# One tile of a depthwise convolution: from GpSimd to the tensor engine, by way of four shifted copies in DRAM

## The chip, the core and the metric

The kernel runs on one core of a Trainium2 chip. Its time is the device time of one execution in microseconds (us); less is better. A core has a tensor engine (PE), a vector engine (DVE), a scalar engine (ACT), GpSimd (POOL), and a queue (SP) that only starts DMA transfers; ACT and POOL start a few as well. Each engine works through its own list of instructions in the order in which the program puts them, and waits on semaphores for the others.

## The reference

One layer of a streaming encoder, for 512 tokens of width 1024, all in float32. A convolution module and an attention module run on one projected input, share one output projection, and a mixture of 32 experts follows. The part that changes is the depthwise convolution over time, 31 taps for each of 512 channels, causal:

```
CONV_CH = 512; CONV_K = 31; SEQ = 512
proj = h @ w_in
conv_val, conv_gate, c_q, c_kv, k_rope = jnp.split(proj, [o1, o2, o3, o4], axis=-1)
...
u  = val * jax.nn.sigmoid(gate)
dw = lax.conv_general_dilated(u, kern, window_strides=(1,), padding=[(CONV_K - 1, 0)],
        dimension_numbers=("NWC", "WIO", "NWC"), feature_group_count=CONV_CH) + conv_b
y_conv = jax.nn.silu(layer_norm(dw, ln_g, ln_b))
...
mixed = jnp.concatenate([y_conv, y_attn], axis=-1) @ w_out
x = x + g_a[:, None] * mixed
return x + g_f[:, None] * hier_moe(rms_norm(x) modulated ...)     # 32 experts, top 2 of one group
```

## The kernel before

The 512 channels are four tiles of 128 channels on the partitions, with time (512) along the row. `conv_in(t, pv, pg)` forms `u` of tile t from two PSUM banks (value and gate): ACT takes a tanh (L312), DVE forms (tanh + 1) * value (L318, or L315 for the tensor engine's tile). The taps of the four tiles are shared out:

- Tiles 0 and 2 are DVE's: `conv_taps` is 31 instructions a tile (L343, L345), each a multiply-add over 128x512. They are put between other DVE work a few at a time by calls of `tap(n)`.
- Tile 1 is GpSimd's: in `conv_taps_pool` ACT multiplies a shifted slice by its tap (L355), GpSimd adds the product to `dw` (L357); 30 adds and 31 ACT instructions, put in by `tap(n, ptaps)`: 3 after each of the four steps of `conv_pair(2)`, 2 after each step of `conv_pair(3)`, and 1 with each of the first attention scores.
- Tile 3 is the tensor engine's: `conv_in` stores `u` to a DRAM buffer `ud` (L316, a DMA on ACT's queue), `load_rep` loads four copies of it, each shifted by one more step, onto the four quarters of the partitions (L325, four DMAs on SP's queue), and `conv_mm` runs 8 steps of four matmuls of 128x32 by 512 (L333), each step covering four taps. The bank is evicted by ACT (L336). The tap weights for it are spread over 32x32 blocks once, by GpSimd (`cwb`, L304).

The order of the program around this: a sweep over the input projection fills tiles 0's banks and the latent columns; then `conv_pair(1)`, `conv_pair(2)`, `conv_pair(3)` compute the value and gate banks of tiles 1 to 3 (16 steps of three matmuls each, L117 to L119). Between their steps stand single steps of `ada_rest` (matmuls L585, whose 1 MB weight pieces SP loads one after another into a ring of four buffers, L511), `c_chunk(0)` to `c_chunk(2)`, and the DVE taps. A `c_chunk` is four PE transposes into a bank of the two-bank pool `tr` (L643), an ACT eviction (L646), an ACT cast (L647) and a DVE subtraction (L648). `pair_split(3)`, two ACT casts (L378) and two DVE subtractions (L379), stands before `conv_pair(2)` in the program and makes the weights that `conv_pair(3)` uses. After `conv_pair(3)` come four rounds of `qkv_mm`/`qkv_tr` (keys, queries and values of 128 tokens: DVE L762 to L785 with taps between them, GpSimd's rotary products L550 to L553 and a root L194), then 32 steps of attention: `scores` (PE L877, DVE L878 and L879, ACT L881), `p_tr` (PE L891), and after every eighth step `attn_out` (PE L901, L909). From the eighth step on the output weights are split (DVE L839, GpSimd L841). Then the output projection, the routing and the experts, whose weights stream in over SP's queue as buffers come free.

PE, DVE, ACT, SP and (up to the end of attention) POOL run in the order of the program. A DMA that an engine's queue starts stands in that engine's order too: the queue goes on only when the DMA's semaphores are there.

Of the kernel before, what the change touches and what calls it, by code (L numbers as in the profile page):

```python
# [37 lines left out]
CONV_POOL, CONV_PE = (1,), 3  # L38
# [3 lines left out]
def hybrid_block(ctx: ExitStack, tc: tile.TileContext, A, out, dbg=None, stop=None):  # L42
# [31 lines left out]
    PP2, PP3, PPQ, PPA = 3, 2, 0, 1  # L74
# [214 lines left out]
    u = S([128, 3, 542])  # L289

    ud = dram.tile([129, 544], F32, tag="ud", name="ud")
    cwb = S([128, 32, 32])
    rep = []

    def conv_setup():
        zz = rp[:, 512:608]
        pool.memset(zz, 0.0)
        pool.dma_start(ud[:, :32].rearrange("(p a) b -> p a b", a=3), zz[:43].rearrange("p (a b) -> p a b", a=3))
# [5 lines left out]
        pool.tensor_tensor(cwb, m32[:, None, :].to_broadcast([128, 32, 32]),  # L304
                           col("cwp")[:, :, None].to_broadcast([128, 32, 32]), op=OP.mult)
# [15 lines left out]
    def load_rep():  # L321
        rep.append(C([128, 4, 540], name="u", uname="rep"))
        flat = ud.rearrange("a b -> (a b)")
        for i in range(4):
            sp.dma_start(rep[0][32 * i:32 * i + 32],  # L325
                         flat[2 + i:2 + i + 128 * 544].rearrange("(g c s) -> c g s", c=32, s=544)[:, :, :540])

    def conv_mm():

        p = fb()  # L330
        for k in range(8):
            for g in range(4):
                pe.matmul(p[32 * g:32 * g + 32, :], cwb[:, 8 * g + k, :], rep[0][:, g, 4 * k:4 * k + 512],  # L333
                          start=(k == 0), stop=(k == 7), tile_position=(0, 32 * g), skip_group_check=True)
            if k == 7:
                act.activation(dw[:, CONV_PE, :], p, AF.Identity, bias=col("cb", CONV_PE, CONV_PE + 1))  # L336
            yield

    def conv_taps(t):
        for k in range(31):  # L340
            w = cwh[:, 31 * t + k:31 * t + k + 1]
            if k == 0:
                dve.tensor_scalar(dw[:, t, :], u[:, t, 0:512], w, col("cb", t, t + 1), op0=OP.mult, op1=OP.add)  # L343
            else:
                dve.scalar_tensor_tensor(dw[:, t, :], u[:, t, k:k + 512], w, dw[:, t, :], op0=OP.mult, op1=OP.add)  # L345
            yield

    def conv_taps_pool(t):

        z = [rp[:, 0:512], rp[:, 896:1408]]  # L350
        for k in range(32):
            if k == 0:
                act.activation(dw[:, t, :], u[:, t, 0:512], AF.Identity, scale=cwh[:, 31 * t:31 * t + 1], bias=col("cb", t, t + 1))
            elif k < 31:
                act.activation(z[k % 2], u[:, t, k:k + 512], AF.Copy, scale=cwh[:, 31 * t + k:31 * t + k + 1])  # L355
            if k > 1:
                pool.tensor_tensor(dw[:, t, :], dw[:, t, :], z[(k - 1) % 2], op=OP.add)  # L357
            yield

    taps, ptaps = [], []  # L360

    def tap(n, q=None):
        q = taps if q is None else q
# [293 lines left out]
    for k in range(4):  # L657
        run(g, 4)
        fill(F2[k])
        if k < 3:  # L660
            c_chunk(k)
        tap(P2)
        tap(PP2, ptaps)
    run(g)
    g = conv_pair(3)
    for k in range(4):
# [3 lines left out]
        tap(PP3, ptaps)  # L670
    run(g)

# [136 lines left out]
    conv_steps, CM = conv_mm(), (0, 1, 1, 0)  # L809
# [5 lines left out]
    for tt in range(4):  # L815
        nxt_ = qkv_mm(tt + 1, g) if tt < 3 else None
        if tt == REP_AT:
            load_rep()
# [3 lines left out]
        tap(PPQ, ptaps)  # L822
# [831 lines left out]
def pack(inputs):  # L1654
# [73 lines left out]
```

## Time and profile before

| | before |
|---|---|
| median of three runs (lowest, highest) | 550.88 us (549.04, 552.13) |
| the profiled execution, its span | 550.6 us, 549.0 us |
| PE busy | 486.6 us, 89% |
| DVE busy | 298.5 us, 54% |
| ACT busy | 197.3 us, 36% |
| POOL busy | 169.2 us, 31% |
| HBM read | 149.84 MB |

The span runs from the first to the last instruction; 1.6 us of the time lie outside it. Busy shares are means over stages with different limits, and PE's busy time is modelled, so a busy PE is not PE at its peak. All times in rows below are from the start of the span.

### The profile page before, as it was taken

The page shows a single profiled execution, that of the slowest core. Times are in us where ns is not written, and L with a number is a line of the kernel's source. Part 1 is how long each engine was busy: PE and PEld are TensorE (multiplying, and loading weights), DVE is VectorE, ACT ScalarE, POOL GpSimd, SP SyncE. Part 2 cuts the span into 40 slices and gives each one's busy share as a digit, 9 for nine tenths or more (in the row PEclk, how much of TensorE's full clock was granted, in tenths as well). Part 3 has the DMA queues.
Part 4 walks back from the last instruction along what each step waited for, and adds up shares of the span by engine and source line. Part 5 has one row for each costly group of instructions (what it writes and reads, how often), then busy time and mean ns, then how long its engine had stood idle before and what let it go on. Part 6 is the DMA issues. An engine that isn't in the chain of part 4 may idle for free.

```text
span 549.0 us, 8137 instructions
## 1 busy us (share of the span) xinstructions
PE 486.6 (89%) x2827; PEld 277.8 (51%) x2827; DVE 298.5 (54%) x631; ACT 197.3 (36%) x419; POOL 169.2 (31%) x147
## 2 busy tenths in 40 slices
PE   4999999948988979999998999999999789989962
PEld 3778865534643446688884443443434332424321
DVE  2447699998998676662456333436433231415532
ACT  4233754534578556752443513112221020211000
POOL 3110674975889563110000213112221120101100
PEclk9999999968999889999999989999999989999988
DMA  8999536935971234266959889999999999999972
GB/s 249 299 347 304 182 131 257 381 113 179 231 217 67 78 93 149 78 236 213 367 180 382 291 346 335 347 409 413 373 414 408 410 411 415 408 410 303 327 296 96
DMA packets 60946, 153.00 MB, mean 279 GB/s; under 512 B 7485, under 2 KB 27085, under 8 KB 55264
## 3 DMA queue, kind: packets, MB, share of 16 engines
q1 hardware_dynamic: 57712, 145.91, 74.7%
q0 software_dynamic: 1792, 3.97, 2.1%
q10 hardware_dynamic: 1392, 2.51, 1.3%
q8 instruction: 24, 0.39, 0.3%
q14 instruction: 26, 0.21, 0.1%
HBM read 149.84 MB, written 4.49 MB: 281 GB/s over the span
## 4 chain that ended last, share of the span: by engine, by line
PE 46%; DVE 23%; DMA 20%; ACT 3%; SPq 3%; issue 2%; POOL 1%; ACTq 0%; DVEq 0%; POOLq 0%
DVE dw L345 10%; PE acc L1480 10%; DMA s<-in_w_up_e_dram 9%; PE acc L1506 6%; PE f L1523 5%; DMA w<-in_w_up_e_dram 4%; PE acc L117 4%; PE acc L119 3%; PE acc L118 3%; DMA w<-in_w_down_e_dram 3%; DMA s<-in_w_down_e_dram 2%; DMA s<-in_w_ada_dram 2%; PE acc L909 2%; DVE sm L879 2%; PE acc L877 1%
## 5 line engine op out<-in xcount | busy, mean ns | idle before, releaser
L1480 PE MATMUL acc<-s,gw 128*32 128x512 f32 (+1 forms) x392 | 93.3, 604 | 1.5 <-DMA s<-in_w_up_e_dram 1.5
L117 PE MATMUL acc<-s,s 128*128 128x512 f32 (+3 forms) x160 | 64.8, 405 | 10.7 <-DVE s L318 8.2
L345 DVE SCALAR_TENSOR_TENSOR dw<-s,cwh,dw 128x512 f32<-128x512 f32 x60 | 63.6, 1061 | 1.5
L119 PE MATMUL acc<-s,s 128*128 128x512 f32 (+3 forms) x160 | 60.1, 376 | 1.4 <-DVE s L379 1.4
L118 PE MATMUL acc<-s,s 128*128 128x512 f32 (+3 forms) x160 | 60.1, 376 | 0.0
L1523 PE MATMUL f<-s,t 128*128 128x512 f32 x184 | 48.7, 412 | 10.8 <-DVE t L1462 8.1
L1480 PE MATMUL acc<-w,gw 128*32 128x512 f32 (+1 forms) x136 | 53.5, 619 | 4.1 <-DMA w<-in_w_up_e_dram 4.0
L1485 DVE TENSOR_TENSOR t<-t,acc 128x256 f32<-128x256 f32 x12 | 5.1, 421 | 91.0 <-ACT t L1483 91.0
L1511 POOL TENSOR_TENSOR s<-t,s 128x512 fp32r<-128x512 f32 x22 | 28.5, 1295 | 75.9 <-ACT s L1510 75.9
L1483 ACT ACTIVATE t<-acc 128x256 f32<-128x256 f32 x12 | 4.6, 384 | 127.8 <-PE acc L1480 127.8
L1480 PEld LDWEIGHTS acc<-s,gw 128*32 128x32 f32 (+1 forms) x392 | 25.8, 123 | 47.9 <-issue 46.4
L357 POOL TENSOR_TENSOR dw<-dw,s 128x512 f32<-128x512 f32 x30 | 45.6, 1518 | 13.1 <-ACT s L355 11.4
L1526 DVE TENSOR_TENSOR s<-s,f 128x512 f32<-128x512 f32 x52 | 35.2, 687 | 20.0 <-PE f L1523 20.0
L1506 PE MATMUL acc<-s,t 128*32 128x512 f32 (+1 forms) x200 | 45.3, 609 | 0.5 <-ACT t L1494 0.5
L1523 PEld LDWEIGHTS f<-s,t 128*128 128x128 f32 x184 | 31.1, 188 | 26.9 <-DVE s L1526 7.3
L1438 POOL DMA_INDIRECT s<-xg,sidx x11 | 11.2, 1020 | 106.9 <-PE tr L1454 65.5
L117 PEld LDWEIGHTS acc<-s,s 128*128 128x128 f32 x160 | 31.1, 194 | 25.2 <-DVE s L318 8.6
L1510 ACT CAST s<-t 128x512 fp32r<-128x512 f32 x24 | 14.8, 618 | 54.8 <-DVE t L1509 54.8
L119 PEld LDWEIGHTS acc<-s,s 128*128 128x128 f32 x160 | 31.1, 194 | 5.9 <-DVE s L379 1.8
L118 PEld LDWEIGHTS acc<-s,s 128*128 128x128 f32 x160 | 31.2, 195 | 3.4 <-issue 0.2
L1509 DVE SCALAR_TENSOR_TENSOR t<-acc,rt,gw 128x512 f32<-128x512 f32 x24 | 18.0, 751 | 27.0 <-PE acc L1506 27.0
L881 ACT ACTIVATE t<-acc,sm,qs 128x128 f32<-128x128 f32 (+3 forms) x32 | 19.7, 616 | 19.9 <-DVE sm L879 16.6
(313 smaller groups left out, 856.1 us busy)
## 6 DMA issues: line engine op xcount, KB each, us to landing
s<-in_w_down_e_dram SPq DMA_DIRECT2D x21, 1024.0 KB
s<-in_w_gate_e_dram SPq DMA_DIRECT2D x41, 512.0 KB
s<-in_w_up_e_dram SPq DMA_DIRECT2D x41, 512.0 KB
w<-in_w_ada_dram SPq DMA_DIRECT2D x16, 1024.0 KB
w<-in_w_gate_e_dram SPq DMA_DIRECT2D x15, 512.0 KB
w<-in_w_up_e_dram SPq DMA_DIRECT2D x15, 512.0 KB
w<-in_w_down_e_dram SPq DMA_DIRECT2D x7, 1024.0 KB
s<-in_w_ada_dram SPq DMA_DIRECT2D x6, 1024.0 KB
```

The costliest lines, as they stand in the source:

```text
L117: pe.matmul(o, lh, rh, start=start, stop=False)
L118: pe.matmul(o, lh, rl, start=False, stop=False)
L119: pe.matmul(o, ll, rh, start=False, stop=stop)
L345: dve.scalar_tensor_tensor(dw[:, t, :], u[:, t, k:k + 512], w, dw[:, t, :], op0=OP.mult, op1=OP.add)
L357: pool.tensor_tensor(dw[:, t, :], dw[:, t, :], z[(k - 1) % 2], op=OP.add)
L881: act.activation(e[:, :n], p[:, :n], AF.Exp, scale=qs[:, qt, h:h + 1], bias=H["nb"][:, qt:qt + 1], accum_out=H["rs"][:, qt:qt + 1])
L1480: pe.matmul(gu[sl, :], self.hg[:, j, sl], w.t[:, :, j % 4, :], start=(j == 0), stop=(j == 7), tile_position=(0, o_), skip_group_check=True)
L1506: pe.matmul(o[o_:o_ + w_, :], self.aT[:, n * c + o_:n * c + o_ + w_], w.t[:, c, hs], start=(c == 0), stop=(c == 1), tile_position=(0, o_), ...
L1509: dve.scalar_tensor_tensor(yf[:n], o[:n], self.gate, gf[:n, hs], op0=OP.mult, op1=OP.mult)
L1511: eng.tensor_tensor(self.yhl[:n, 1, hs], yf[:n], self.yhl[:n, 0, hs].bitcast(F32), op=OP.subtract)
L1523: pe.matmul(o, u_.ot[:u_.n, tt * 128:(tt + 1) * 128], u_.yhl[:u_.n, k, 512 * hf:512 * hf + 512], start=(m == 0 and k == 0), stop=(m == len ...
L1526: dve.tensor_tensor(xr, xr, o, op=OP.add)
```

## The change

Tile 1 is treated as tile 3 was. `conv_taps_pool` and its queue go, with all 30 adds of GpSimd and 31 instructions of ACT. `conv_in(1)` now forms `u` in a temporary and stores it to a second DRAM buffer, `ud1`; four loads on SP fill `rep1`; `conv_mm(1)` runs right after `conv_pair(3)`, all 8 steps in one piece. The block weights `cwb` double, from 128x1024 to 128x2048. `rep1` and `rep3` share one buffer in SBUF. DVE's two tiles stay.

```diff
-CONV_POOL, CONV_PE = (1,), 3
+CONV_PE = 1, 3
...
     def conv_in(t, pv, pg):
...
-        if t == CONV_PE:
+        if t in CONV_PE:
             ut = T()
             dve.scalar_tensor_tensor(ut, th, 1.0, pv, op0=OP.add, op1=OP.mult)
-            act.dma_start(ud[:128, 32:], ut)
+            act.dma_start(ud[t][:128, 32:], ut)
             return
-        dve.scalar_tensor_tensor(u[:, t, 30:], th, 1.0, pv, op0=OP.add, op1=OP.mult)
-        (ptaps.append(conv_taps_pool(t)) if t in CONV_POOL else taps.append(conv_taps(t)))
+        dve.scalar_tensor_tensor(u[:, t // 2, 30:], th, 1.0, pv, op0=OP.add, op1=OP.mult)
+        taps.append(conv_taps(t))
...
-    def conv_taps_pool(t):
-        z = [rp[:, 0:512], rp[:, 896:1408]]
-        for k in range(32):
-            if k == 0:
-                act.activation(dw[:, t, :], u[:, t, 0:512], AF.Identity, scale=cwh[:, 31 * t:31 * t + 1], bias=col("cb", t, t + 1))
-            elif k < 31:
-                act.activation(z[k % 2], u[:, t, k:k + 512], AF.Copy, scale=cwh[:, 31 * t + k:31 * t + k + 1])
-            if k > 1:
-                pool.tensor_tensor(dw[:, t, :], dw[:, t, :], z[(k - 1) % 2], op=OP.add)
-            yield
...
     g = conv_pair(2)
     for k in range(4):
         run(g, 4)
         fill(F2[k])
         if k < 3:
             c_chunk(k)
+        if k == 2:
+            load_rep(1)
         tap(P2)
-        tap(PP2, ptaps)
     run(g)
     g = conv_pair(3)
+    conv_steps = conv_mm(1)
     for k in range(4):
         run(g, 4)
         fill(F3[k])
         tap(P3)
-        tap(PP3, ptaps)
     run(g)
+    run(conv_steps)
...
             scores(i // 4, i % 4)
             tap(PT)
-            tap(PPA, ptaps)
```

On ACT, behind the tanh of tile 1 (t_766 before, t_768 now), stood the casts of `pair_split(3)` (s_773) and the eviction and cast of `c_chunk(0)` (tr_797), then the first products of GpSimd's tile. Before:

```order
L312 ACTIVATE t_766<-f_701 128x512
L378 CAST s_773<-w_574 128x1024 x2
L646 ACTIVATE t_802<-tr_797,smalls 128x512
L647 CAST s_634<-t_802 128x512
L353 ACTIVATE dw<-s_147,smalls,cwh 128x512
L355 ACTIVATE s_146<-s_147,cwh 128x512 x2
L646 ACTIVATE t_836<-tr_831,smalls 128x512
```

And of the change, the same place:

```order
L312 ACTIVATE t_768<-f_703 128x512
L316 DMA ud_148<-t_770 128x512
L367 CAST s_777<-w_576 128x1024 x2
L635 ACTIVATE t_806<-tr_801,smalls 128x512
L636 CAST s_636<-t_806 128x512
L635 ACTIVATE t_836<-tr_831,smalls 128x512
```

The store of `u` of tile 1 (t_770, which DVE writes) now stands ahead of the casts and of the first `c_chunk`'s eviction, and the products of GpSimd's tile are gone.

On PE, at the end of `conv_pair(3)` (acc_905), the matmuls of `conv_mm(1)` come ahead of the first key matmuls of `qkv_mm` (acc_1048). Of the change:

```order
L574 MATMUL f_988<-w_959,cs 32x512 x4
L116 MATMUL acc_905<-s_140,s_777 128x512
L117 MATMUL acc_905<-s_142,s_777 128x512
L118 MATMUL acc_905<-s_140,s_778 128x512
L334 MATMUL f_1006<-rep_870,s_150 32x512 x32
L116 MATMUL acc_1048<-s_692,s_636 128x512
```

In the kernel before the last three matmuls of `conv_pair(3)` and the key matmuls follow each other directly; the 32 in one row are new.

On SP, the loads of `rep1` (rep_870) stand among the 1 MB pieces of `ada_rest`. Of the change:

```order
L500 DMA w_859<-in_w_ada_dram 128x2048
L325 DMA rep_870<-ud_148 32x4x540 x4
L500 DMA w_894<-in_w_ada_dram 128x2048
L500 DMA w_919<-in_w_ada_dram 128x2048
L500 DMA w_939<-in_w_ada_dram 128x2048
```

Before, the pieces followed each other with nothing between; the loads of `rep3` stay where those of `rep` were.

## Rows read from the trace of the kernel before

**Rows 1.** The page's fourth part: shares of the chain that ended last

```profile
DVE dw L345 10%; PE acc L1480 10%; DMA s<-in_w_up_e_dram 9%; PE acc L1506 6%; PE f L1523 5%; DMA w<-in_w_up_e_dram 4%; PE acc L117 4%; PE acc L119 3%; PE acc L118 3%; DMA w<-in_w_down_e_dram 3%; DMA s<-in_w_down_e_dram 2%; DMA s<-in_w_ada_dram 2%; PE acc L909 2%; DVE sm L879 2%; PE acc L877 1%
```

**Rows 2.** DVE and POOL in the timeline: start, length, line, operation, [idle before]

```profile
69.77 17.07 DVE L345 SCALAR_TENSOR_TENSOR dw<-s,cwh,dw 128x512 f32<-128x512 f32 x15
86.76 0.68 DVE L318 SCALAR_TENSOR_TENSOR s<-t,f 128x512 f32<-128x512 f32 x1
...
91.30 4.53 DVE L379 TENSOR_TENSOR s<-w,s 128x1024 fp32r<-128x1024 f32 x2
...
97.45 5.17 DVE L345 SCALAR_TENSOR_TENSOR dw<-s,cwh,dw 128x512 f32<-128x512 f32 x3
...
120.93 5.47 DVE L345 SCALAR_TENSOR_TENSOR dw<-s,cwh,dw 128x512 f32<-128x512 f32 x7
...
88.98 31.62 POOL L357 TENSOR_TENSOR dw<-dw,s 128x512 f32<-128x512 f32 x18 [9.78 <-ACT s L355]
```

**Rows 3.** PE in the timeline, 76 to 125 us

```profile
86.54 0.65 PE L643 MATMUL tr<-ident,t 128*128 128x128 f32 x4
...
93.66 0.50 PE L119 MATMUL acc<-s,s 128*128 128x512 f32 x1 [1.36 <-DVE s L379]
...
109.28 1.06 PE L585 MATMUL f<-w,cs 128*32 128x512 f32 x8
110.27 0.50 PE L117 MATMUL acc<-s,s 128*128 128x512 f32 x1
...
120.14 0.69 PE L117 MATMUL acc<-s,s 128*128 128x384 f32 x1 [8.20 <-DVE s L318]
...
124.27 1.48 PE L585 MATMUL f<-w,cs 128*32 128x512 f32 x8
```

**Rows 4.** ACT in the timeline (ACTq: a DMA that its queue starts)

```profile
75.10 1.98 ACT L378 CAST s<-w 128x1024 fp32r<-128x1024 f32 x2
78.22 0.69 ACT L646 ACTIVATE t<-tr,smalls 128x512 f32<-128x512 f32 x1 [1.14 <-PE tr L643]
...
127.03 0.37 ACTq L316 DMA_DIRECT2D ud<-t  x1
127.45 0.60 ACT L759 ACTIVATE t<-acc 128x512 f32<-128x512 f32 x1 [7.28 <-DVE t L315]
```

**Rows 5.** Windows: length, busy us of PE, PEld, DVE, ACT, POOL, granted clock, DMA

```profile
114.00:116.00 2.00, 0.00 (x0) 0.00 (x0) 1.96 (x2) 1.05 (x2) 1.92 (x2) 0.73 0.00 0
...
124.00:126.00 2.00, 1.75 (x10) 0.20 (x8) 1.89 (x4) 0.00 (x0) 0.00 (x0) 0.71 0.51 213
```

**Rows 6.** SP's queue in the timeline, the four loads of `rep`

```profile
137.60 4.62 SPq L325 DMA_DIRECT2D rep<-ud  x4
```

**Rows 7.** POOL and DVE in the timeline, the first `qkv_mm`

```profile
129.26 1.22 POOL L550 TENSOR_TENSOR t<-s,s 128x256 f32<-128x256 f32 x1 [8.65 <-DVE sm L190]
...
135.00 0.69 DVE L783 TENSOR_TENSOR s<-acc,ks 128x512 f32<-128x512 f32 x1 [1.08 <-POOL ks L194]
```

**Rows 8.** POOL in the timeline, its first work behind the block weights

```profile
56.94 6.17 POOL L379 TENSOR_TENSOR s<-w,s 128x1024 fp32r<-128x1024 f32 x2 [17.66 <-ACT s L378]
```

**Rows 9.** PE in the timeline, attention: scores of steps 4, 12, 20, 28, and one `attn_out`

```profile
165.62 0.49 PE L877 MATMUL acc<-s,s 100*128 100x128 f32 x2
...
181.36 0.80 PE L877 MATMUL acc<-s,s 100*128 100x128 f32 x2
...
199.02 0.41 PE L877 MATMUL acc<-s,s 100*128 100x128 f32 x2
...
200.44 1.98 PE L901 MATMUL tr<-ident,rec 128*64 128x128 f32 x16 [0.68 <-DVE s L892]
...
205.18 0.70 PE L877 MATMUL acc<-s,s 100*128 100x256 f32 x2
...
215.19 0.39 PE L877 MATMUL acc<-s,s 100*128 100x128 f32 x2
```

**Rows 10.** Waits of SP's queue, longest first: us in total, times, longest

```profile
SPq L1008 <- POOL s L841: 40.2, 3, 22.5
```

More of the change, by code (lines that the diff above doesn't have):

```diff
@@ L73, in hybrid_block @@
     P2, P3, PQ = 3, 2, 2
-    PP2, PP3, PPQ, PPA = 3, 2, 0, 1
     REP_AT = 1
@@ L288, in hybrid_block @@
     rp = S([128, 2048])
[L289 to L293, printed above, removed]
+    u = S([128, 2, 542])
+    ud = {t: dram.tile([129, 544], F32, tag=f"ud{t}", name=f"ud{t}") for t in CONV_PE}
+    cwb = S([128, 64, 32])
+    rep = {}
     def conv_setup():
@@ L297, in conv_setup @@
         pool.memset(zz, 0.0)
-        pool.dma_start(ud[:, :32].rearrange("(p a) b -> p a b", a=3), zz[:43].rearrange("p (a b) -> p a b", a=3))
+        for t in CONV_PE:
+            pool.dma_start(ud[t][:, :32].rearrange("(p a) b -> p a b", a=3), zz[:43].rearrange("p (a b) -> p a b", a=3))
         m32 = rp[:, 608:640]
@@ L303, in conv_setup @@
         dve.tensor_scalar(m32, m32, 0.5, None, op0=OP.mult)
-        pool.tensor_tensor(cwb, m32[:, None, :].to_broadcast([128, 32, 32]),
-                           col("cwp")[:, :, None].to_broadcast([128, 32, 32]), op=OP.mult)
+        pool.tensor_tensor(cwb, m32[:, None, :].to_broadcast([128, 64, 32]),
+                           col("cwp")[:, :, None].to_broadcast([128, 64, 32]), op=OP.mult)
     def conv_in(t, pv, pg):
@@ L312, in conv_in, with load_rep, conv_mm @@
         act.activation(th, pg, AF.Tanh, scale=0.5)
-        if t == CONV_PE:
+        if t in CONV_PE:
             ut = T()
             dve.scalar_tensor_tensor(ut, th, 1.0, pv, op0=OP.add, op1=OP.mult)
-            act.dma_start(ud[:128, 32:], ut)
+            act.dma_start(ud[t][:128, 32:], ut)
             return
-        dve.scalar_tensor_tensor(u[:, t, 30:], th, 1.0, pv, op0=OP.add, op1=OP.mult)
-        (ptaps.append(conv_taps_pool(t)) if t in CONV_POOL else taps.append(conv_taps(t)))
-    def load_rep():
-        rep.append(C([128, 4, 540], name="u", uname="rep"))
-        flat = ud.rearrange("a b -> (a b)")
+        dve.scalar_tensor_tensor(u[:, t // 2, 30:], th, 1.0, pv, op0=OP.add, op1=OP.mult)
+        taps.append(conv_taps(t))
+    def load_rep(t):
+        rep[t] = C([128, 4, 540], name="u", uname=f"rep{t}")
+        flat = ud[t].rearrange("a b -> (a b)")
         for i in range(4):
-            sp.dma_start(rep[0][32 * i:32 * i + 32],
+            sp.dma_start(rep[t][32 * i:32 * i + 32],
                          flat[2 + i:2 + i + 128 * 544].rearrange("(g c s) -> c g s", c=32, s=544)[:, :, :540])
-    def conv_mm():
+    def conv_mm(t):
+        w0 = 32 * CONV_PE.index(t)
         p = fb()
@@ L332, in conv_mm @@
             for g in range(4):
-                pe.matmul(p[32 * g:32 * g + 32, :], cwb[:, 8 * g + k, :], rep[0][:, g, 4 * k:4 * k + 512],
+                pe.matmul(p[32 * g:32 * g + 32, :], cwb[:, w0 + 8 * g + k, :], rep[t][:, g, 4 * k:4 * k + 512],
                           start=(k == 0), stop=(k == 7), tile_position=(0, 32 * g), skip_group_check=True)
             if k == 7:
-                act.activation(dw[:, CONV_PE, :], p, AF.Identity, bias=col("cb", CONV_PE, CONV_PE + 1))
+                act.activation(dw[:, t, :], p, AF.Identity, bias=col("cb", t, t + 1))
             yield
@@ L342, in conv_taps, with tap @@
             if k == 0:
[L343 removed]
+                dve.tensor_scalar(dw[:, t, :], u[:, t // 2, 0:512], w, col("cb", t, t + 1), op0=OP.mult, op1=OP.add)
             else:
[L345 removed]
+                dve.scalar_tensor_tensor(dw[:, t, :], u[:, t // 2, k:k + 512], w, dw[:, t, :], op0=OP.mult, op1=OP.add)
             yield
[L348 to L363 removed]
+    taps = []
+    def tap(n):
+        q = taps
         while n and q:
@@ L807, in qkv_tr @@
                 yield i
-    conv_steps, CM = conv_mm(), (0, 1, 1, 0)
+    conv_steps, CM = conv_mm(3), (0, 1, 1, 0)
     QS = 3
@@ L817, in hybrid_block @@
         if tt == REP_AT:
-            load_rep()
+            load_rep(3)
         tap(PQ if tt < 3 else T3[2])
@@ L821, in hybrid_block @@
             run(conv_steps, CM[0])
-        tap(PPQ, ptaps)
         for i, _ in enumerate(qkv_tr(tt, tok)):
@@ L1677, in pack @@
     put("cw", cw.transpose(2, 1, 0).reshape(128, 124))
-    cp = np.zeros((32, 4, 32), np.float32)
-    cp[:31] = cw[:, CONV_PE].reshape(31, 4, 32)
-    put("cwp", cp.reshape(8, 4, 4, 32).transpose(1, 3, 2, 0).reshape(128, 32))
+    cps = []
+    for t in CONV_PE:
+        cp = np.zeros((32, 4, 32), np.float32)
+        cp[:31] = cw[:, t].reshape(31, 4, 32)
+        cps.append(cp.reshape(8, 4, 4, 32).transpose(1, 3, 2, 0).reshape(128, 32))
+    put("cwp", np.concatenate(cps, 1))
     put("qa", nat(g["q_a_norm"][0]))
```

2 lines of the change are left out of this document (1 added, 1 removed).

## The prediction

> **What bounds the kernel now.** I read the page's chain first, then the timelines of DVE, POOL, PE and ACT over one stretch, 60 to 230 us, because outside it the change touches only some preparation before 40 us. In the chain the reader should see that DVE's taps and the expert matmuls lead with a tenth of the span each, and that the expert weights (the DMA entries) come next [rows 1]: there is no one bound, each stage has its own. GpSimd's adds do not appear in the chain at all. What the change can save must therefore come through something that they hold up.
>
> They hold up DVE. While GpSimd adds, from 88.98 for 31.62 us, three of DVE's taps take 5.17 us, 1.72 each; when GpSimd rests, seven take 5.47 us, 0.78 each [rows 2]. Because DVE is late, PE stands for 8.20 us in front of 120.14, waiting for DVE's L318, and then works at half clock [rows 3]: the granted clock was already falling in 114 to 116, with PE idle, and only in 124 to 126 it was on its way back [rows 5].
>
> **The change, step by step.** I follow the in-order lists through this stretch, on the profiled execution (550.6 us; the median of the runs, 550.88, is 0.3 above it, which I neglect).
>
> *DVE.* Between 95.8 and 119.4 stand 14 instructions of 128x512 (11 taps, 3 subtractions of `c_chunk`) at about 1.7, which come to about 0.78: 14 x 0.92 = 12.9 us, and the two L379 take 4.53 now [rows 2] and some 2.5 without company (an estimate: two of twice a tap's length less a fixed part). DVE gets some 15 us of room. But what stands behind its taps waits for PE, so this room is worth only what PE's order lets through.
>
> *The store moved ahead on ACT.* ACT's queue now holds at the store of `ud1` until DVE has written tile 1, and that is L318 at 86.76, behind 15 taps [rows 2]. Nothing of GpSimd's tile slows these 15 taps, so they stay where they are. Queued behind the store are the two casts of `pair_split(3)` and the eviction of `c_chunk(0)`, which ran at 75.10 and 78.22 [rows 4]. Now: 86.76 + 0.68 = 87.44, store 0.37, casts 1.98, eviction 0.69 [rows 2, 4], so `c_chunk(0)` leaves its bank at 90.5. The transposes of `c_chunk(2)` need that bank, since the pool has two, and PE reached them at 86.54 [rows 3]. PE is in order, so it stands there for 4.0 us. That the queue really holds is in the trace: behind the store of tile 3, ACT stood for 7.28 us on DVE's L315 [rows 4].
>
> *The clock.* A pause of 4 us may let the clock fall. Before, PE stood for 8.20 us, and with the clock at half until about 125 it worked some 5 us at 1.2 GHz after 120.14, worth 2.5 us [rows 3, 5]. The new pause is half as long and the work behind it denser: bounds 0 (no fall) and 2.5, and I take 1.7, nearer to the row of a pause that did cost. The Trainium skill, in "TensorE: Matmul & The Clock Gate", Part 1, says that the throttled state is the default and that sustained activity alone releases it, which speaks against a change that puts a new hole into a stretch where PE had none; by it the term would be the full 2.5 and the sum 0.8 us worse. The trace agrees in kind (0.73 in 114 to 116) [rows 5].
>
> *What falls away on PE.* `conv_pair(3)` stood 1.36 us for L379 [rows 3]. PE now comes there some 5.7 us later and DVE is done by 93, so the wait goes. `conv_pair(3)` therefore ends at about 111.1 + 4.0 + 1.7 - 1.4 = 115.4 (its last three matmuls start at 110.27 [rows 3] and take 0.8).
>
> *The 32 matmuls.* One step of four has the shape of an L585 step, which takes 0.99 us from start to start (109.28 to 110.27 [rows 3]): 8 x 0.99 = 7.9 us, to 123.3. They fill the 8.20 us in which PE stood for DVE. Without that cover they would cost the full 7.9. Their input: `rep1` can start when the store has landed, which no row times; from below nothing, from above the four loads of `rep`, issued over 4.62 us from 137.60 [rows 6] and used without a wait at 156.5, so at most 19 us. Issued at about 91, `rep1` is there by 110 at the worst, ahead of 115.4. The 1 MB pieces behind it on SP are needed from about 104 on; the same bound lets one of them be late by 2 us at most, and I take 0.
>
> *The first `qkv_mm`.* Keys 0.8, then twelve query matmuls, which took 120.14 to 124.27 at half clock [rows 3] and take about 2.1 at full: PE has them at 126.2. ACT copies them in about 0.6, and GpSimd's rotary products, at 129.26 before, start at 126.8: 2.5 us earlier. They release L783 on DVE, at 135.00 before [rows 7]. From there up to attention DVE is the bound in both kernels, with the same work, so the lead is kept: **front part 2.5 us, bounds 0.5 and 4.3** (clock term and 1 us either way in the pause).
>
> *Attention.* Steps 4 to 12 took 15.7 us with GpSimd's adds and ACT's products among them (165.62 to 181.36); steps 20 to 28, with neither, and almost without splitting of output weights, 16.2 less one `attn_out` of 4.7 (200.44 to 205.18), so 11.4 [rows 9]. The gain is between 0 and 4.3. The four casts and subtractions of the output weights in it stay, and so do the matmuls of tile 3, so I take half, 2.0, and 0.6 for steps 0 to 4: **2.6 us, bounds 0 and 5**.
>
> *Costed at nothing:* the doubled `cwb` on GpSimd, since GpSimd stands 17.66 us before its next work at 56.94 [rows 8]; the second clearing store beside it; 16 KB more of small inputs. If that cover were gone, the price would be about one GpSimd instruction of 128x1024, 3.1 us [rows 8].
>
> *Behind attention* everything is released by work that moves along: the first expert loads wait 40.2 us in three waits for GpSimd's L841 [rows 10]. So the lead arrives whole at the end. Sum: 550.6 - 2.5 - 2.6 = **545.5 us**.
>
> **The rivals.** *All of DVE's room counts.* If PE did not bind from 86 to 123, 15 us of front and 2.6 of attention would come through: 533. For it speaks that DVE's taps lead the chain [rows 1]; against it, that PE stands only 1.36 and 8.20 us in the whole stretch [rows 3], and 4.0 plus 7.9 are put in. The Trainium skill, in "SBUF — State Buffer", Who interferes with whom, has the shared read port held for a whole instruction by a DVE operation with two SBUF inputs or by GpSimd, the loser blocked; by that the 15 us are truly freed on DVE. The trace agrees (1.72 against 0.78). A part of this, down to 541, is possible if the pause is shorter. Chance 0.10.
>
> *The lead is lost on the way:* the clock stays down longer than 2.5 us are worth, attention keeps its pace because PE's own work sets it (0 from rows 9's lower bound), or the weight stream of the last 300 us does not move. Front 0.5, attention 0: 550.1. Chance 0.20.
>
> *Slower: the taps do not quicken.* If DVE's 1.72 has another cause than GpSimd, DVE still reaches L318 of tile 2 at about 119.5, then eight more taps at 1.7, and L315 at 133. The second store on ACT holds the queue until then, with the eviction of `conv_mm(1)` and the key squares behind it: 133.7 instead of 127.45, 6.2 us later, less 2.6 in attention: 554.2. It decides once L315 comes after 124. Against it speak the seven taps at 0.78 with DMA running beside them [rows 2, 5]. Chance 0.07; for causes that I do not see, above 553, another 0.06.
>
> **How the numbers follow.** The forecast, 541.5 to 548.1, has 0.57. I count 0.5% (2.75 us), about what a measurement of this kernel can tell from no change, as the border: faster is below 548.1, slower above 553.6. Faster: 0.57 + 0.10 = 0.67; within: 0.20; slower: 0.13. The range reaches from a half unit of the first rival to the lost lead: 540 to 551, leaving out the deep first rival (0.07) and what is slower than the lost lead (0.13).
>
> **What the next profile would show.** Right: ACT's first store of `ud1` at about 87.4, PE waiting some 4 us for ACT in front of the third group of `c_chunk` transposes, the clock at half for some microseconds behind it; DVE's taps at 0.78 from 90 on, and DVE idle before the tanh of tile 3; the 32 matmuls from about 115 without a wait for DMA; L783's like at about 132.5; steps 4 to 12 of attention in 13 to 14 us. Wrong: PE idle in front of the 32 matmuls (`rep1` late), waits of L585's like for weights, taps above 1 us with GpSimd at rest, a front that gains while attention or the weight stream gives it back.

## The result

The changed kernel takes 544.44 us (median of 7 runs, 542.37 to 546.93) against 550.88 for the kernel before beside it (7 runs, 549.04 to 553.31): ratio 0.9892, 95% interval 0.9861 to 0.9922, so 6.4 us faster. A second set of 12 runs gave 545.87, ratio 0.9901 (0.9865 to 0.9937). The prediction was 545.5. The profiled execution has a span of 541.3 us.

**Where the time went.** Because the start of the program scatters by some microseconds, I cut every profile at four places that all kernels have: A, the first group of `c_chunk` transposes on PE; B, the first scores; C, the first `attn_out`; D, the 16 matmuls of PE on the routing weights, behind the last `attn_out` (L1072 before, at 235.14 us; L1061 after, at 230.03). Stretches in us, each a difference of two starts in the timeline:

| | A | A to B | B to C | C to D | D to end |
|---|---|---|---|---|---|
| before | 77.47 | 82.69 | 22.57 | 52.41 | 313.9 |
| after | 79.25 | 80.08 | 18.53 | 52.17 | 311.3 |
| after, second profile | 78.94 | 80.82 | 18.54 | 51.71 | 314.1 |
| store of tile 1 on SP (`e1`) | 81.34 | 75.71 | 18.54 | 51.50 | 312.2 |
| the same, second profile (`e12`) | 78.77 | 75.88 | 18.54 | 53.17 | 311.8 |

The front (A to B) gained 2.6 us, in the second profile 1.9; attention (B to C) gained 4.0 in both; the start lost 1.8 and 1.5, in a stretch that scatters by more than that from run to run. At D the lead is 5.1 us in both profiles. Behind D the same kernel lies 2.8 us apart in its two profiles, so the last 2.6 us of the first profile's 7.7 are within the scatter.

**The profile after.** The page's chain, by engine and by line, to be held against [rows 1] (the page cuts its second line off):

```profile
PE 56%; DMA 19%; DVE 12%; SPq 4%; ACT 4%; issue 2%; POOL 2%; ACTq 0%; DVEq 0%
PE acc L1469 10%; PE acc L1495 6%; DMA s<-in_w_up_e_dram 6%; PE f L1512 5%; PE acc L116 5%; DMA s<-in_w_down_e_dram 5%; PE acc L117 5%; PE acc L118 5%; DMA w<-in_w_up_e_dram 4%; DVE dw L346 3%; DMA s<-in_w_ada_dram 2%; PE f L334 2%; SPq L16
```

DVE's taps no longer lead it: L346 has 3% of the span, where L345 had 10%. The next lines are the timelines of DVE, PE and ACT (start, length, engine, line, operation, [idle before]) that answer to [rows 2 to 4]. DVE:

```profile
88.52 0.68 DVE L315 SCALAR_TENSOR_TENSOR t<-t,f 128x512 f32<-128x512 f32 x1
89.12 3.10 DVE L346 SCALAR_TENSOR_TENSOR dw<-s,cwh,dw 128x512 f32<-128x512 f32 x4
92.14 2.35 DVE L368 TENSOR_TENSOR s<-w,s 128x1024 fp32r<-128x1024 f32 x2
...
104.50 0.68 DVE L318 SCALAR_TENSOR_TENSOR s<-t,acc 128x512 f32<-128x512 f32 x1
...
117.57 0.69 DVE L315 SCALAR_TENSOR_TENSOR t<-t,acc 128x512 f32<-128x512 f32 x1 [6.30 <-ACT t L312]
...
132.88 0.69 DVE L774 TENSOR_TENSOR s<-acc,ks 128x512 f32<-128x512 f32 x1 [2.32 <-POOL ks L193]
```

PE, and ACT (ACTq is a DMA that its queue starts):

```profile
87.33 1.06 PE L574 MATMUL f<-w,cs 128*32 128x512 f32 x8
92.27 0.72 PE L632 MATMUL tr<-ident,t 128*128 128x128 f32 x4 [3.87 <-ACT t L635]
...
115.94 0.50 PE L116 MATMUL acc<-s,s 128*128 128x512 f32 x1
116.84 7.07 PE L334 MATMUL f<-rep,s 128*32 128x512 f32 x64
123.84 0.50 PE L116 MATMUL acc<-s,s 128*128 128x512 f32 x1
```

```profile
89.24 0.36 ACTq L316 DMA_DIRECT2D ud<-t  x1
89.64 1.99 ACT L367 CAST s<-w 128x1024 fp32r<-128x1024 f32 x2 [12.66 <-DVE t L315]
91.54 0.68 ACT L635 ACTIVATE t<-tr,smalls 128x512 f32<-128x512 f32 x1
```

Four taps now take 3.10 us, 0.78 each, and the two subtractions 2.35 instead of 4.53. DVE is early enough that it twice stands for more than 6 us (6.30 in front of 117.57, and 6.6 in front of its first sums of the keys). The price stands in the other two: ACT's queue holds for 12.66 us until DVE's tile 1 is there, and PE therefore waits 3.87 us in front of the third group of transposes. Behind this pause the granted clock falls to 0.50, that is 1.2 GHz; for [rows 5] the same view (windows: length, busy us of PE, PEld, DVE, ACT, POOL, clock, DMA):

```profile
90.00:92.00 2.00, 0.00 (x0) 0.00 (x0) 1.93 (x3) 2.00 (x3) 0.00 (x0) 1.00 0.35 131
92.00:94.00 2.00, 1.73 (x7) 1.51 (x8) 2.00 (x3) 1.94 (x4) 0.00 (x0) 0.68 0.79 205
94.00:96.00 2.00, 2.00 (x6) 1.54 (x5) 1.97 (x4) 1.31 (x3) 0.00 (x0) 0.50 1.04 211
96.00:98.00 2.00, 2.00 (x13) 0.83 (x12) 1.97 (x4) 0.00 (x0) 0.00 (x0) 0.96 1.14 236
```

The 32 matmuls of tile 1 (the trace records each twice) run for 7.0 us from 116.84 without a wait, in the place of the former 8.20 us of waiting [rows 3].

### The profile page after: what moved, and what is told of

It reads as the page before. It is cut to its first block, busy times and chain, and to the rows that moved or that the text cites. A ratio compares the mean times of both kernels' runs of the same rounds, so it can differ in the third digit from the quotient of the medians.

```text
span 541.3 us, 8200 instructions
## 1 busy us (share of the span) xinstructions
PE 487.9 (90%) x2891; PEld 277.0 (51%) x2891; DVE 276.4 (51%) x631; ACT 177.8 (33%) x389; POOL 125.5 (23%) x118
## 4 chain that ended last, share of the span: by engine, by line
PE 56%; DMA 19%; DVE 12%; SPq 4%; ACT 4%; issue 2%; POOL 2%; ACTq 0%; DVEq 0%
PE acc L1469 10%; PE acc L1495 6%; DMA s<-in_w_up_e_dram 6%; PE f L1512 5%; PE acc L116 5%; DMA s<-in_w_down_e_dram 5%; PE acc L117 5%; PE acc L118 5%; DMA w<-in_w_up_e_dram 4%; DVE dw L346 3%; DMA s<-in_w_ada_dram 2%; PE f L334 2%; SPq L167 2%; DMA w<-in_w_ada_dram 2%; PE acc L899 2%
## 5 line engine op out<-in xcount | busy, mean ns | idle before, releaser
L116 PE MATMUL acc<-s,s 128*128 128x512 f32 (+3 forms) x160 | 63.8, 399 | 1.0 <-DVE s L774 1.0
L117 PE MATMUL acc<-s,s 128*128 128x512 f32 (+3 forms) x160 | 59.4, 371 | 0.0
L118 PE MATMUL acc<-s,s 128*128 128x512 f32 (+3 forms) x160 | 59.3, 370 | 0.0
L1469 PE MATMUL acc<-w,gw 128*32 128x512 f32 (+1 forms) x136 | 52.0, 595 | 3.5 <-DMA w<-in_w_up_e_dram 3.4
L346 DVE SCALAR_TENSOR_TENSOR dw<-s,cwh,dw 128x512 f32<-128x512 f32 x60 | 51.8, 863 | 1.5
L1474 DVE TENSOR_TENSOR t<-t,acc 128x256 f32<-128x256 f32 x12 | 5.1, 421 | 90.4 <-ACT t L1472 90.4
L116 PEld LDWEIGHTS acc<-s,s 128*128 128x128 f32 x160 | 30.5, 190 | 14.9 <-issue 7.9
L118 PEld LDWEIGHTS acc<-s,s 128*128 128x128 f32 x160 | 30.5, 191 | 4.2
L117 PEld LDWEIGHTS acc<-s,s 128*128 128x128 f32 x160 | 30.6, 191 | 3.4 <-issue 0.2
L1499 ACT CAST s<-t 128x512 fp32r<-128x512 f32 x24 | 14.8, 619 | 53.2 <-DVE t L1498 53.2
L868 DVE TENSOR_REDUCE sm<-acc 128x1 f32<-128x128 f32 (+3 forms) x32 | 15.5, 485 | 18.2 <-PE acc L867 18.1
```

Source lines behind the costliest of these rows:

```text
L116: pe.matmul(o, lh, rh, start=start, stop=False)
L117: pe.matmul(o, lh, rl, start=False, stop=False)
L118: pe.matmul(o, ll, rh, start=False, stop=stop)
L346: dve.scalar_tensor_tensor(dw[:, t, :], u[:, t // 2, k:k + 512], w, dw[:, t, :], op0=OP.mult, op1=OP.add)
L868: dve.tensor_reduce(H["mx"][:, qt:qt + 1], p[:, :n], axis=AX.X, op=OP.max)
L1469: pe.matmul(gu[sl, :], self.hg[:, j, sl], w.t[:, :, j % 4, :], start=(j == 0), stop=(j == 7), tile_position=(0, o_), skip_group_check=True)
```

## The experiments

All are one edit of the changed kernel, or, where it says so, of the kernel before. Times are medians; ratios are to runs of the kernel before beside them (medians 549.64, 551.95 and 550.58 in the three sets).

**e1 and e12: without the hold on ACT.** Tile 1's store goes to SP's queue, right ahead of the loads of `rep1`:

```diff
-            act.dma_start(ud[t][:128, 32:], ut)
+            if t == 1:
+                held.append(ut)
+            else:
+                act.dma_start(ud[t][:128, 32:], ut)
...
     def load_rep(t):
+        if t == 1:
+            sp.dma_start(ud[t][:128, 32:], held.pop())
```

> The changed kernel with one edit: the store of tile 1 is issued from SP, straight ahead of the four loads of rep1, no longer from ACT's queue. The prediction's theory (the hold of ACT's queue is what stops PE for 3.87 us and then halves its clock): the casts of pair_split(3) and the eviction of c_chunk(0) return to about 77 to 80 us, PE has no wait in front of the third group of c_chunk transposes, the clock stays full from 88 to 98, and conv_pair(3), the 32 matmuls of tile 1 and the first queries stand 5 to 5.5 us earlier than in the changed kernel; all of it reaches the end: 539 to 540 us against 544.4. Rival (DVE sets the end of this stretch, its taps of tile 2 running to 111): the tanh of tile 3 cannot be taken up earlier than 111.3, queries gain 5 us at most on PE but the key squares less, 542 to 543. Rival (the new wait on SP, store and then loads behind each other, makes rep1 or the 1 MB pieces behind it late): PE stands in front of the 32 matmuls or of the L574 steps, 544 or slower.

> The kernel of e1 once more, beside the changed kernel. In the profile of e1 it led the changed kernel by 5.0 us from the first group of c_chunk transposes to the end of attention, but its median only by 1.8 us against the kernel before's. If the 5 us are whole at the end: 539 to 540 here, and e1's profile (first group of transposes at 81.3 us instead of 79.3) fell on a late start. If something behind attention takes them back, or the start is late whenever this edit is made: 541 to 543.

Measured: 541.44 us, ratio 0.9878 (0.9831 to 0.9924), and again 541.45, ratio 0.9843 (0.9788 to 0.9897), beside 545.87 for the changed kernel in the same set. PE has no wait in front of the transposes, and the clock is 1.00 from 86 to 98. From A to the 32 matmuls e1 takes 33.7 us (changed kernel: 37.6), not 32.3 as the 5 to 5.5 us that I expected would give, because a smaller wait, for a piece of `w_ada`, came in its place. PE's timeline of e1:

```profile
103.26 1.06 PE L581 MATMUL f<-w,cs 128*32 128x512 f32 x8 [1.33 <-DMA w<-in_w_ada_dram]
```

SP now stands at the store until 91.33 and at the loads behind it until 93.65, and the 1 MB pieces follow at 95.49. That is 14.2 us behind A, hardly later than in the changed kernel (93.23, 14.0 behind A): it is PE that comes to them earlier. A to B is 4.4 us shorter than in the changed kernel (4.9 in the second pair of profiles). So the rival that DVE sets the end did not hold (in e1 DVE stands 2.48 us for ACT's tanh in front of tile 3), and the one of a new wait held in part.

How much of the 4.4 us reaches the end is less sure. In the set that holds both kernels the medians are 541.45 and 545.87, 4.4 us apart. In the first set e1 was only 1.8 us better than the changed kernel by the differences to the kernel before, and the lead of e1 and e12 over the changed kernel's two profiles is 2.9 and 3.7 us at D, with starts and stretches C to D that scatter. By its number e12 fell into the range that I had set for a loss (541 to 543, not 539 to 540), but the changed kernel beside it was slower too, and the stretch behind D shows no loss (311.8 against 314.1).

**e10: the store on GpSimd's queue, the loads of `rep1` one step later.**

```diff
-            act.dma_start(ud[t][:128, 32:], ut)
+            (pool if t == 1 else act).dma_start(ud[t][:128, 32:], ut)
...
-        if k == 2:
+        if k == 3:
             load_rep(1)
```

> The changed kernel with two edits: tile 1's store is issued from GpSimd, which is idle there, and the loads of rep1 stand one step later in SP's order (behind one more 1 MB piece of w_ada). In e1 SP itself waited for DVE's tile 1 and then for the store, and PE stood 1.3 us for a piece of w_ada at 103.3. Theory: neither that wait nor the hold on ACT is left; from the first group of c_chunk transposes to the 32 matmuls 32.3 to 32.6 us (the changed kernel 37.6, e1 33.7), to the first scores 74 to 75 (80.1, 75.7); time 539.5 to 541. Rival: rep1, issued later, is late: PE waits for DMA in front of the 32 matmuls, and the gain against e1 is lost.

Measured: 541.35 us, ratio 0.9855 (0.9805 to 0.9905), the same as e12 beside it; A to B 77.4 us, longer than e1's. The theory of a wait that SP's order alone makes fell: A to the 32 matmuls took 34.2 us instead of 32.3 to 32.6, and PE waited again for pieces of `w_ada`, now four times, but not for `rep1`. The view of waits (us in total, times, longest):

```profile
PE f L574 <- DMA w<-in_w_ada_dram: 3.2, 4, 1.6
```

With the hold gone PE comes to these pieces so early that their transfers are the next limit, whoever issues the store; that is read from the waits of e1, e12 and e10, and no run moved the pieces themselves.

**e8: only the clock.** 14 matmuls that nothing reads fill PE's pause:

```diff
+        if k == 2:
+            pz = fb()
+            for i in range(14):
+                pe.matmul(pz, pair_w[2][0][:, 0, i % 8, :], hTh[0][:, 0, :], start=True, stop=True)
         if k < 3:
             c_chunk(k)
```

> The changed kernel plus 14 matmuls of 128x512 (3.2 us at full clock) into a free bank, straight ahead of the third group of c_chunk transposes, where PE stands for 3.87 us; what they write is read by nothing. They change nothing but what PE does in the pause. Theory (the pause lets the clock fall, and the half clock behind it costs 1.4 us or so): granted clock 1.00 from 88 to 98, the triples behind the transposes at 0.23 us for a matmul and not 0.43, and from the first group of transposes to the 32 matmuls 36.0 to 36.4 us instead of 37.6, about 543 us against 544.4. Rival (the matmuls behind the pause are slow for another reason, such as DMA traffic): still 0.43, still 37.6 us, 544.4. If the 14 matmuls last longer than the pause, the third group is late by the difference.

Measured: the clock stays up behind the pause. The windows of e8, columns as above:

```profile
92.00:94.00 2.00, 2.00 (x12) 1.65 (x11) 2.00 (x2) 1.97 (x4) 0.00 (x0) 1.00 0.83 221
94.00:96.00 2.00, 2.00 (x12) 1.15 (x14) 1.97 (x4) 1.03 (x2) 0.00 (x0) 1.00 1.06 210
```

From A to the 32 matmuls it is 36.3 us instead of 37.6. The 14 matmuls overran the pause by 0.3 us (the transposes start 13.4 us behind A, 13.0 in the changed kernel); from the transposes to the 32 matmuls it is 22.9 us instead of 24.6. The half clock behind the pause thus costs 1.6 us. The time, 544.63 us, ratio 0.9886 (0.9850 to 0.9921), cannot show so little.

**e2: all that GpSimd's tile cost.** An edit of the kernel before; of tile 1 only the first tap is left:

```diff
-        for k in range(32):
+        for k in range(1):
```

> The kernel before with one edit: of tile 1 only the first tap is computed, by ACT; ACT's other 30 products and GpSimd's 30 adds are left out, and nothing takes their place on PE. It prices all that GpSimd's tile cost. My theory (the adds hold up DVE, and PE's new work then takes most of that room back): taps at 0.78 us throughout, PE's waits of 1.36 and 8.20 us and the half clock behind them go, the first queries start some 13 us earlier than before, and attention's steps 4 to 12 take about 12 us instead of 15.7: 550.9 - 13 - 4 = 534 us, so some 10 us under the changed kernel. Rival (something else, such as the w_ada pieces or the bank of conv_pair(3), stands behind PE's wait): the front gains under 5 us and the time is 541 to 545, no better than the changed kernel.

Measured: A to B 67.0 us instead of 82.7, B to C 18.5 instead of 22.6, 535.33 us, ratio 0.9756 (0.9713 to 0.9800). The left-out taps alter the numbers from which the experts are chosen, so behind D this time isn't comparable (317.5 us there); the stretches ahead of D are. GpSimd's tile had thus cost 15.7 us in the front and 4.0 in attention. PE's new work gives 13.1 of the 15.7 back (13.8 in the changed kernel's second profile). Added up from the other readings these are 3.9 of pause, 1.6 of clock, 7.0 for the 32 matmuls, and a remaining 0.6 in the query rounds and elsewhere; pause and clock have runs of their own, the split of the rest is arithmetic.

**e4: GpSimd's company alone.** 18 adds on GpSimd into a scratch tile return to the front, without ACT's products; the first reads tile 1, so that they start where they did:

```diff
...
+    def idle_adds(n):
+        for _ in range(n):
+            x = first.pop() if len(first) == 1 and not begun else u[:, 0, 30:]
+            begun.append(1)
+            pool.tensor_tensor(zd, zd, x, op=OP.add)
...
+        idle_adds((1, 3, 3, 3)[k])
         tap(P2)
...
+        idle_adds(2)
         tap(P3)
```

> The changed kernel plus 18 adds of 128x512 on GpSimd into a scratch tile that nothing reads, in GpSimd's order where the kernel before had its 18 adds of the front, the first behind DVE's tile 1; no ACT products. It brings back GpSimd's company for DVE and nothing else. If GpSimd's adds are what slows DVE: taps between 90 and 120 at 1.6 to 1.75 us while the adds run, tile 2 of DVE done some 8 to 12 us late, the tanh product of tile 3 behind it, the eviction of the 32 matmuls and the key squares held on ACT until then: 550 to 556 us against 544.4, that is slower than the changed kernel and near the kernel before. Rival (DVE's 1.72 came from ACT's products or from the tile's data, not from GpSimd): taps stay at 0.78, 544 to 545.

Measured: 546.31 us, ratio 0.9931 (0.9897 to 0.9966), A to B 84.1 us (80.1 without the adds). DVE and POOL in its timeline:

```profile
99.87 4.58 DVE L348 SCALAR_TENSOR_TENSOR dw<-s,cwh,dw 128x512 f32<-128x512 f32 x3
...
125.35 0.68 DVE L316 SCALAR_TENSOR_TENSOR t<-t,acc 128x512 f32<-128x512 f32 x1
...
90.91 26.50 POOL L358 TENSOR_TENSOR s<-s,s 128x512 f32<-128x512 f32 x17
```

The taps are at 1.53 us each while GpSimd adds, so its company does slow DVE, a little less than I said (before: 1.72 [rows 2]; what makes the rest stays open). Tile 3 is 7.8 us late on DVE, as expected, but the time grew by about 2 us only, not by 5 to 10: ACT, held until then, worked off its evictions in a row, and GpSimd's first rotary product starts at 128.84 instead of 127.51. The profile itself is dearer than the medians: its A to B is 4.1 us longer than the changed kernel's (3.3 than the second profile's), so the price lies between 2 and 4 us.

**e3: attention without GpSimd's tile.** An edit of the kernel before; its last 12 taps of tile 1 are left out:

```diff
-    PP2, PP3, PPQ, PPA = 3, 2, 0, 1
+    PP2, PP3, PPQ, PPA = 3, 2, 0, 0
```

> The kernel before with one edit: the last 12 taps of GpSimd's tile, all of those that stand in attention (ACT's products and GpSimd's adds), are left out; the front stays as it was. If attention's gain in the changed kernel comes from these alone: steps 4 to 12 in 11.8 to 12.5 us instead of 15.7, the rest unchanged: 550.9 - 3.7 = 547 us. Rival (attention went faster in the changed kernel for another reason, such as the weight pieces arriving earlier): steps 4 to 12 stay at 15 to 16 us, 550 to 551.

Measured: B to C 18.53 us, as in the changed kernel to 0.01 us, and the front unchanged (A to B 82.6). So attention's 4.0 us come from these taps alone. The time, 605.72 us, tells nothing: as in e2 the left-out taps reach the choice of experts, and here the stretch behind D takes 371.9 us (its page has 17 loads of `w_gate` into `w` tiles, the kernel before 15).

**e6, e7, e9: which part of these taps.** 12 adds on GpSimd, 12 products on ACT, or both with each add reading the product before, return to the first score steps of the changed kernel; nothing else reads what they write. The adds of e6 (e7 has an `act.activation` of the same size in their place, e9 both):

```diff
...
             tap(PT)
+            if i < 12:
+                pool.tensor_tensor(zd, zd, u[:, 0, 30:], op=OP.add)
```

> The changed kernel plus 12 adds of 128x512 on GpSimd into a scratch tile that nothing reads, one behind each of the first 12 score steps, where the kernel before had its last 12 adds; no products on ACT. From the first scores to the first attn_out the kernel before took 22.6 us, all kernels without adds and products 18.5. If GpSimd's company for DVE makes the difference: 21 to 22.6 us and 2.5 to 4 us on the time (547 to 548.5). If ACT's products in the line of exponentials make it: 18.5 to 19.5 us, 544 to 545.5.

> The changed kernel plus 12 products of 128x512 on ACT into the same scratch tile, one behind each of the first 12 score steps, where the kernel before had its last products; no adds on GpSimd. If ACT's products in the line of exponentials make attention's difference of 4.0 us: 21 to 22.6 us from the first scores to the first attn_out; if GpSimd's adds make it: 18.5 to 19.5 us. In the kernel before ACT had no gap from 162.5 to 172.6 us and waited for DVE behind that, so I expect both to hold a part, this one 1 to 2 us (545.5 to 546.5).

> The changed kernel plus 12 products on ACT and 12 adds on GpSimd in the first 13 score steps, each add reading the product of the step before, as in the kernel before; what they write is read by nothing else. Alone, the adds made the stretch from the first scores to the first attn_out 20.2 us and the products 19.1, instead of 18.5; the kernel before took 22.6. If the two only add up: 20.8 us. If they hold each other up (an add waits for its product, a product for the buffer that an add still reads, and the exponentials stand behind it on ACT): 22 to 22.8 us, and the whole 4.0 us is explained; time 547 to 549.

Measured from B to C: adds 20.24 us, products 19.13, both 19.66; the kernel before 22.57, none 18.53. Times 545.96, 547.37 and 546.71 us (ratios 0.9901, 0.9917, 0.9939, each known to 0.35% either way). All three expectations of a large part for one cause, or of the whole for both, fell: the two together bring back 1.1 of 4.0 us, less than the adds alone (1.7). What differs in the kernel before is in DVE's groups of 160 to 184 us (busy us, mean ns of one). Before:

```profile
L839 DVE CAST s<-w 128x512 fp32r<-128x512 f32 x5 | 5.2, 1036 | 0.0
L878 DVE TENSOR_REDUCE sm<-acc 128x1 f32<-128x512 f32 x3 | 2.0, 682 | 0.4 <-PE acc L877 0.4
```

After:

```profile
L829 DVE CAST s<-w 128x512 fp32r<-128x512 f32 x6 | 2.4, 407 | 0.0
L868 DVE TENSOR_REDUCE sm<-acc 128x1 f32<-128x512 f32 x3 | 2.1, 687 | 0.5 <-PE acc L867 0.4
```

Beside GpSimd's adds three of these five casts of output weights took 1.4 to 1.5 us instead of 0.41, while the reductions kept their length. The Trainium skill, "SBUF — State Buffer", Who interferes with whom, says just this: casts and instructions with two SBUF inputs can meet GpSimd at the shared port, reductions never; the trace agrees. In e6 and in e9 two casts were caught, and PE's clock stayed at 1.00; in the kernel before it fell to half as well, at the end of this stretch. The window of the kernel before:

```profile
180.00:182.00 2.00, 2.00 (x11) 0.64 (x4) 1.85 (x4) 0.74 (x2) 2.00 (x3) 0.50 0.00 0
```

That the missing 2.9 us are the third caught cast and this half clock is read from the traces, not shown by a run.

**e5: the 32 matmuls elsewhere.** The store on SP as in e1, and the eight steps spread over the first two query rounds; the loads for tile 3 one round later:

```diff
-    REP_AT = 1
+    REP_AT = 2
...
-    run(conv_steps)
...
             run(g, 1)
+            if tt < 2:
+                run(conv1, 1)
```

> The changed kernel with two edits: tile 1's store issued from SP as in e1, and the eight steps of the 32 matmuls of tile 1 no longer in one piece between conv_pair(3) and the keys, but one behind each query and key transposition of the first two row tiles; the loads of rep for tile 3 move one row tile later. Theory (on PE the 32 matmuls cost their full 7.0 us where DVE and ACT have nothing to do, as DVE's idle 6.5 us in front of the first key sums shows; between 128 and 160 us DVE is the bound and PE has room for them): from the third group of transposes to the first scores the kernel takes 5 to 6 us less than e1 (e1: 75.7 us from the first group of transposes to the first scores; here 70 to 71), 536 to 537 us against 541.4. Rival (PE has no room there either; each step delays the transposes behind it): 75 us and 541. Rival (the later rep of tile 3 makes PE wait in the fourth row tile): a DMA wait of some us in front of its matmuls, 538 to 541.

Measured: 543.42 us, ratio 0.9869 (0.9832 to 0.9905), A to B 76.4 us against e1's 75.7. The first keys come 6.5 us earlier on DVE (A to L774's like 43.2 us, e1 49.7), and all of it is gone at B. The windows of the query rounds:

```profile
124.00:134.00 10.00, 10.00 (x74) 4.38 (x75) 8.88 (x18) 3.55 (x6) 7.75 (x7) 1.00 0.92 314
134.00:144.00 10.00, 10.00 (x77) 4.51 (x75) 9.50 (x16) 4.96 (x10) 6.86 (x6) 1.00 0.71 204
```

PE is busy without a gap in these 20 us. My theory that DVE is the bound there and PE has room fell; the rival holds. The other rival, of a late `rep` for tile 3, held in small: PE waits 0.9 us for it in the fourth round.

**e11: the changed kernel again**, for the scatter of a single profile.

> The changed kernel once more, beside e10 and e12 on the same chip. From the first group of c_chunk transposes to the first scores 80.1 us, from there to the first attn_out 18.5 us; time 544 to 545. If the start (first group at 77.5 to 81.7 us in the profiles so far) and the end scatter as they did, single executions lie 2 us either way.

Measured: 545.87 us (12 runs, 541.01 to 550.18), a little above the 544 to 545 that I expected; its stretches stand in the first table. Over the twelve profiles of kernels that leave nothing out, C to D lies between 50.6 and 53.2 us and D to the end between 311.3 and 314.1, in no order that the edits explain.

## Why the prediction was right

The time, the range and the mechanism held: tile 1's taps were a load on DVE, and PE's order let only a part of the freed time through. Step by step, with times of the changed kernel moved to the kernel before's A (less 1.78 us):

- *DVE.* Right: taps at 0.78 from 87 on, and DVE idle for 6.30 us before tile 3 instead of late.
- *The store on ACT.* Right: `c_chunk(0)` was forecast to leave its bank at 90.5 and left it at 90.4; pause 4.0 forecast, 3.87 measured. e1 shows that the store's place is the cause and what it is worth up to attention: 4.4 us (4.9 in the second pair), pause and clock together.
- *The clock.* Right: 1.7 us forecast, 1.6 measured by e8. The full term of 2.5 us, which the prediction had from its own rows and set beside its choice by the rule of the Trainium skill ("TensorE: Matmul & The Clock Gate", Part 1), was too much for this pause.
- *What falls away, and the 32 matmuls.* The 1.36 us wait went, and `rep1` was in time. The matmuls cost 7.0 us, not 7.9; they ran closer than the step that I took for a model [rows 3].
- *The lead kept to attention.* This step failed. GpSimd's first product came 3.5 us earlier (forecast 2.5) and the first product of the keys 3.9, but only 2.6 and 1.9 us were left at B. I had said that DVE is the bound in the query rounds in both kernels. In the kernel before it is: the chain of work that ended last (start, length, engine) runs over DVE alone from 135.00 to 159.22, here its end:

```profile
155.91 0.66 DVE dw L345
...
158.15 0.64 DVE s L783
```

  In the changed kernel the chain runs over PE and a piece of `w_ada` (SP can load it when PE has freed its buffer, at 136.5), then over ACT and GpSimd, and back to PE:

```profile
136.52 9.75 DMA w<-in_w_ada_dram
146.31 1.06 PE f L574 x8
...
151.39 0.48 ACT s L763
...
153.07 1.33 POOL t L541 x2
...
155.89 0.99 PE f L334 x8
```

  The loss is in the fourth round alone: its product of the keys comes 8.3 us behind the third's, before 6.6. GpSimd, which stood 0.70 us for ACT's copies of the queries there, stands 3.08 us, and DVE, which did not wait, stands 1.07 us for GpSimd (2.71 in the second profile). Before, and after:

```profile
152.50 1.30 POOL L550 TENSOR_TENSOR t<-s,s 128x256 f32<-128x256 f32 x1 [0.70 <-ACT s L772]
```

```profile
152.39 0.73 POOL L539 TENSOR_TENSOR t<-s,s 128x256 f32<-128x256 f32 x1 [3.08 <-ACT t L765]
157.28 0.69 DVE L774 TENSOR_TENSOR s<-acc,ks 128x512 f32<-128x512 f32 x1 [1.07 <-POOL ks L193]
```

  So PE, with its weights, is the bound of that round; this is read from the two traces, and no run isolates it. e5 shows how full PE is in the rounds ahead of it. The front's sum of 2.5 us came out right by luck: the first product of the keys was 1.4 us earlier than forecast (131.1, not 132.5), the matmuls' 0.9 among them, and 1.3 us were then lost.
- *Attention.* Right in kind, mis-sized: 2.6 us forecast, 4.0 measured, within the bounds of 0 to 5. I had taken half of a difference of steps. The trace had rows that bear on it and that I did not use: the caught casts of L839 and the clock of 0.50 at 180 us.
- *Costed at nothing.* This failed for the second clearing store. I looked for its price on GpSimd, which has room [rows 8], and it lies in the DMA. The rate of all transfers from 15 to 40 us in slices of 0.625 us, and their sum, before:

```profile
GB/s 305 284 259 321 326 232 157 179 245 324 328 352 357 306 346 349 364 347 330 329 345 357 353 350 351 349 347 349 347 347 343 320 331 347 356 362 344 367 333 349
DMA packets 9373, 8.12 MB, mean 325 GB/s; under 512 B 346, under 2 KB 9367, under 8 KB 9371
```

  After:

```profile
GB/s 267 316 284 280 305 228 188 140 182 283 322 310 326 326 333 351 356 364 345 311 197 90 202 308 354 353 351 351 346 349 349 347 347 336 323 339 348 360 349 357
DMA packets 9002, 7.61 MB, mean 304 GB/s; under 512 B 430, under 2 KB 8992, under 8 KB 9000
```

  One dip (to 157) stands where the kernel before has its one clearing store, and a second one (to 90) at 28 us, behind the second store, issued at 22.12. At 350 GB/s the 0.51 MB that are missing are 1.5 us (an estimate), in a stretch in which PE waits for `w_ada`; A is 1.8 and 1.5 us later. The Trainium skill, "DMA: Bandwidth & Descriptors", Specifications, names 512 bytes as the least piece for full rate; the store's pieces are 128 bytes by the program, and the count under 512 bytes rises by 84. That the second dip belongs to the second store, the other runs bear out: the three profiles with one clearing store (before, e2, e3) have one dip and 8.11 to 8.14 MB in this stretch, the eleven with two have a second one, to between 84 and 174 GB/s, and 7.58 to 7.76 MB. Its price in time is read, not shown: A lies at 77.47, 77.77 and 79.46 us with one store and at 78.77 to 81.76 with two, so the two groups overlap.
- *Behind attention.* Right: the lead of 5.1 us at D, in both profiles, is what the sum said, and it is not lost behind D. That the number is the same is luck in part: attention gave 1.4 us more than its term, and the start, which the sum had at nothing, took 1.8 and 1.5.

Of the rivals, "the taps do not quicken" is refuted by the taps and by e4, which also shows that its price (554.2) was too high: with the taps slow again the time is 2 us more (4 in the profile), not 10. "All of DVE's room counts" (533) is the 15.7 us that e2 shows in the front, and PE's work stands in its way. "The lead is lost on the way" (550.1) is refuted by the times, 544.4 and 545.9, though a part of it came true in the fourth query round.

## What to carry to other kernels

An offload is paid at the receiving engine's order, not by its busy share: follow each instruction that the move adds to a queue, DMA starts above all, to the first engine that waits for what is queued behind it. Here the placing of one store cost 4.4 us up to attention, as much as attention gained; the versions with the store on another queue, 541.4 us in three runs, are the fastest of those that leave nothing out. And a transfer that costs its issuer nothing can still cost the stream that it falls into.

## What the runs showed of the hardware

- A store of 129 rows of 128 bytes from GpSimd's queue took the rate of all transfers from some 350 to 90 to 200 GB/s for about 2 us, though it moves 16 KB; the dip is there in all eleven profiles with a second such store and in none of the three without.
- The start scatters by 4 us (A from 77.47 to 81.76), and the late starts are those with a low clock: the five behind 80 us have 0.66 to 0.85 from 30 to 40 us, the others 0.86 to 1.00. Where PE waited 1.6 us for `w_ada` (before) the clock stayed at 1.00 from 30 to 40 us and A came at 77.47; where it waited 3.4 us (e1) the clock was 0.66 there and A came at 81.34. The length of the wait alone does not decide it: e12 waited 3.2 us, kept 1.00, and has A at 78.77. The window of e1:

```profile
30.00:40.00 10.00, 10.00 (x53) 7.94 (x42) 4.73 (x10) 3.22 (x5) 0.00 (x0) 0.66 1.10 347
```

- The price of GpSimd's company depends on what meets it: a tap went from 0.78 to 1.53 (e4) or 1.72 us (before), a cast from 0.41 to 1.5, a reduction not at all.
